# Gathered rows spread further into the V pass, and a final norm that takes some of its tokens as rows

## The chip, the cores and the metric

The kernel runs on one core of a Trainium2 chip. Its time is the device time of that core in microseconds; lower is better. Several executions are timed and their median is taken, and one execution is recorded by the hardware profiler. The engines are called PE (matrix products), ACT, DVE, POOL (GpSimd) and SP (which here only issues DMAs).

## The reference

The program is a decoder trunk of two layers over 256 tokens of width 1024. The even layer has an attention and a retention mixer, the odd layer a short gated convolution; each mixer is followed by a PEER block, and at the end stands a root-mean-square norm.

```
for layer in range(2):
    xn = rmsnorm(h, norm_mix[layer])
    h = h + (attn_retention_mixer if layer % 2 == 0 else short_conv_mixer)(xn, ...)
    h = h + peer(rmsnorm(h, norm_ffn[layer]), w_q, sub_keys, u, v)
return rmsnorm(h, final_norm)

# peer: per token, 8 heads each choose 16 of 16384 experts (product keys)
hid = gelu(einsum('td,thkd->thk', t, u[eidx]))
out = einsum('thk,thkd->td', gate * hid, v[eidx])

# short_conv_mixer
bg, cg, hx = split(xn @ w_in, 3);  return (bg * conv3(cg * hx)) @ w_out
```

All data are float32.

## The kernel before

**Two ways through PEER.** Each layer splits its 256 tokens. The last 160 (TD) go through all 16384 experts densely: the U pass multiplies 128 tiles of `pu` (128 experts x 1024, 512 KB each) into the hidden values HG, and the V pass multiplies 128 tiles of `pv` with HG into eight PSUM tiles `vo`, each holding 128 of the 1024 columns, transposed. The first 96 tokens (TG) are fetched: their 96 x 128 expert rows are gathered in 96 batches of 128 rows (512 KB) from `pun`, and again 96 from `pv`. One partition of a batch is one expert row. So a layer has 192 batches; the class `Gather` issues them by GpSimd's indirect DMA (L953) into six buffers, and consumes each with one DVE operation: L963 for the U half, L978 (L974 at two borders between quarters) for the V half, which adds the row, times its gate and hidden value, to an accumulator.

**The schedule of the batches.** `Gather.step` is called once a tile. It adds `rate` to a credit and, where the credit has reached one, consumes a batch and issues the next that has a free buffer. At the start of V, `rate` is set so that the batches left are used up after a fixed number of tiles (L1409). After the last batch GpSimd issues a small DMA (`part`, L990) that brings 32 partitions of an accumulator, 128 KB, to the others, and `fold` (L986, two DVE operations on 96 partitions) adds the accumulators to the residual `h`. The second of the two reads what the small DMA wrote. The fold stands at tile NK-5 = 123 of V.

**The tiles of V.** 95 of the 128 tiles are split (list SPL): ACT casts the tile to a rounded high half (L1356), DVE makes the remainder in bf16 (L1363), ACT and DVE do the same for the rows of HG (L1426, L1427, L1434; up to three tiles in one operation), and PE multiplies the halves (L1470, L1472). The other 33 go through in float32 (L1466). Casts run three tiles ahead of PE, remainders two. Raw tiles have eight buffers; even ones are issued by SP, odd ones by ACT. High and low halves have three buffers each. ACT, DVE, POOL and each DMA queue work in the order in which the program was written; nothing is moved by a planner.

**The end of V.** At tiles 16 to 23 PE adds the residual of the 160 dense tokens to `vo` by a product with the identity (L1455, L1456). At tile NK-2 = 126 it transposes the 96 fetched tokens of `h`, after the fold, into a free part of `vo` (L1458), and ACT copies them into the transposed residual XT (L1461). After tile 127 `fold(b)` (ACT L1479, DVE L1480) brings the dense tokens into XT. In the first layer XT feeds the odd mixer. In the last, `Final.folded` transposes XT back with PE (L504) into four tiles `fq`: quarters 0 and 1 are tokens 0 to 127, quarters 2 and 3 tokens 128 to 255. ACT sums the squares of each quarter (L579), DVE multiplies by the gain (L576), `mean0`, `root` and `rstd` (L363, L366, L371 to L375) make the scale of a half, `put` scales a quarter on DVE (L585) or ACT (L583), and SP sends it out (L586).

**The odd mixer.** Its 24 input tiles are split by the class `Stream`: ACT casts (L146) and the remainder is made by GpSimd or DVE (L148), by a flag beside each tile in `srcs`. Before the change GpSimd has the odd tiles from 7 on. PE multiplies the halves (L258, L264), and DVE does the gates and the convolution (L885 to L908).

Of the kernel before, what the change touches and what calls it, by code (L numbers as in the profile page):

```python
# [14 lines left out]
AF = mybir.ActivationFunctionType  # L15
OP = mybir.AluOpType
# [12 lines left out]
NK = 128  # L29
# [162 lines left out]
def trunk_kernel(ctx, tc, x, small, cst, mcst, ew_in, ew_out, ow_in, ow_out, wq, keys, pu, pv, pun, gains, out):  # L192
# [26 lines left out]
    srcs += [(ow_in[f], i > 6 and i % 2 == 1) for i, f in enumerate(OF)]  # L219
# [123 lines left out]
    class Sums:  # L343


        def __init__(self):
            self.w = pers.tile([P, 2, 8], F32, tag="nw", name=nm("nw"))
# [207 lines left out]
    class Final(Sums):  # L555


        def __init__(self, g):
            super().__init__()
            self.g = g  # L560
# [5 lines left out]
        def folded(self, XT, fold):  # L566

            xs = new_ko().rearrange("p (a d) -> p a d", a=2)
# [5 lines left out]

            def gained(a):
                v.tensor_tensor(part(a), fq[a], self.g[:, a % 2 * 512:(a % 2 + 1) * 512], OP.mult)  # L576

            def square(a):
                act.activation(junk, fq[a], AF.Square, accum_out=self.w[:, a // 2, a % 2:a % 2 + 1])  # L579
# [10 lines left out]
            for a in range(4):  # L590
                back(fq[a], XT, a // 2, a % 2)
            for a in range(2):
                square(a)
            self.mean0(0)
            self.root(0)
            gained(0)
            gained(1)
            self.rstd(0)
            for a in range(2, 4):
                square(a)  # L600
            self.mean0(1)
            self.root(1)
            put(0, v)
            gained(2)
            put(1, act)
            gained(3)
            self.rstd(1)
            put(2, v)
            put(3, act)
# [390 lines left out]
    def peer(l, before, norm):  # L1000
        with tc.tile_pool(name=nm("hg"), bufs=1) as hp:
# [407 lines left out]
            ga.rate = (ga.TOTAL - ga.c) / (NK - 10.0)  # L1409
# [29 lines left out]
            for i in range(NK):  # L1439
# [12 lines left out]
                for b in range(ND):  # L1452
                    c = slice(b * P, (b + 1) * P)
                    if i == 16 + b:
                        pe.matmul(vo[b][:, :P - TG], h[:, 0, c], ident[:, TG:], **m)  # L1455
                        pe.matmul(vo[b][:, P - TG:TD], h[:, 1, c], ident, **m)  # L1456
                    if i == NK - 2:
                        pe.matmul(vo[b][:, 2 * TD:2 * TD + TG], h[:, 0, c], ident[:, :TG], **m)  # L1458
                if i == NK - 2:
                    for b in range(ND):  # L1460
                        act.copy(XT[:, b, :TG], vo[b][:, 2 * TD:2 * TD + TG])  # L1461
# [13 lines left out]
                if i == NK - 5:  # L1475
                    assert ga.c == ga.TOTAL
                    ga.fold()
# [65 lines left out]
```

## Time and profile before

| | us |
|---|---|
| median of 3 runs | 1500.05 (1498.83 to 1500.72) |
| the profiled execution, its own time | 1498.47 |
| its span, from the first to the last instruction | 1496.7 |
| V pass of the first layer, PE's first to last product | 488.2 to 756.3 |
| V pass of the second layer | 1215.2 to 1485.5 |

The engines were busy for 1437.2 us (PE), 1251.9 (DVE), 762.7 (ACT) and 729.4 (POOL) of the span. A row of the profile that groups instructions has the line, engine, operation, output and inputs, shape and count, then busy time, the mean of one in ns, and the idle time before them with what ended it. A row of the timeline has start, duration, engine, line, and in brackets the idle time ahead of the instruction with its releaser. A row of a stretch has its limits and length, each engine's busy time with the number of instructions, the granted PE clock as a share, DMA's share and GB/s. A row of the chain has the start, the duration and what the end was waiting for at that time.

### The profile page before, as it was taken

What the parts mean: (1) busy time and instruction counts of PE and PEld (TensorE: products, weight loads), DVE (VectorE), ACT (ScalarE), POOL (GpSimd) and SP (SyncE); (2) the same over time, 40 slices, a digit from 0 to 9 for tenths busy, and PEclk for the clock granted to TensorE, in tenths of its full rate; (3) what the DMA queues carried; (4) which work ended last, traced back from release to release, by engine and by line L of the source; (5) the groups of instructions that cost most, each with busy time, mean ns of one, the idle gap of its engine ahead of it and who ended that gap; (6) DMA issues with size and microseconds to landing.
All of it is one profiled execution on the core that took longest, in us unless ns stands there. A gap on an engine that the chain in (4) does not pass through costs nothing.

```text
span 1496.7 us, 30119 instructions
## 1 busy us (share of the span) xinstructions
PE 1437.2 (96%) x11174; PEld 1336.0 (89%) x11188; DVE 1251.9 (84%) x2469; ACT 762.7 (51%) x1833; POOL 729.4 (49%) x512
## 2 busy tenths in 40 slices
PE   9999999999999999889999999999999999998897
PEld 5667999999999998888888799999999999988886
DVE  5637999879998888888877589996899969888886
ACT  6556512257885544445564463112888744444445
POOL 6754545446666344444125374454666725444430
PEclk9999999999999999999999999999999999999999
DMA  8545899999999999999966488999999999999994
GB/s 322 195 153 200 302 392 408 395 409 405 407 402 408 407 400 409 409 400 408 371 224 200 169 284 327 408 407 397 408 407 401 408 396 407 401 409 400 409 408 170
DMA packets 147570, 532.99 MB, mean 356 GB/s; under 512 B 16992, under 2 KB 17248, under 8 KB 147424
## 3 DMA queue, kind: packets, MB, share of 16 engines
q1 hardware_dynamic: 72144, 258.36, 45.2%
q0 software_dynamic: 56704, 205.07, 34.7%
q10 hardware_dynamic: 18576, 67.64, 11.5%
q8 instruction: 88, 1.44, 0.4%
q14 instruction: 58, 0.48, 0.1%
HBM read 528.34 MB, written 1.05 MB: 354 GB/s over the span
## 4 chain that ended last, share of the span: by engine, by line
PE 47%; DMA 27%; DVE 19%; issue 5%; ACT 3%; POOL 0%; SPq 0%; DVEq 0%; ACTq 0%; POOLq 0%
PE hid L1345 17%; DMA raw<-pv 12%; PE vo L1470 6%; DMA rows<-pun,ig 4%; PE vo L1466 4%; DMA grow<-pv,ig 4%; DMA rows<-pv,ig 3%; PE hid L258 3%; PE vo L1472 3%; DVE rows L963 3%; PE ea L290 2%; PE ea L291 2%; DVE gacc L978 2%; PE ea L292 1%; PE hid L264 1%
## 5 line engine op out<-in xcount | busy, mean ns | idle before, releaser
L1345 PE MATMUL hid<-xf,raw 128*128 128x160 f32 x3392 | 486.6, 301 | 6.3 <-DMA raw<-pu 4.0
L1345 PEld LDWEIGHTS hid<-xf,raw 128*128 128x128 f32 x3392 | 467.0, 191 | 8.9 <-issue 5.6
L1356 ACT CAST vhi<-raw 128x1024 fp32r<-128x1024 f32 x190 | 198.5, 1046 | 272.4 <-DMA raw<-pv 218.2
L1470 PE MATMUL vo<-ko,vhi 128*128 128x320 f32 x1520 | 271.6, 321 | 33.2 <-DVE ko L1434 32.8
L953 POOL DMA_INDIRECT rows<-pv,ig x128 | 186.2, 1455 | 214.0 <-DVE gacc L978 174.7
L1363 DVE TENSOR_TENSOR vlo<-raw,vhi 128x1024 bf16<-128x1024 f32 x190 | 231.5, 1222 | 63.9 <-ACT vhi L1356 51.0
L1470 PEld LDWEIGHTS vo<-ko,vhi 128*128 128x128 f32 x1520 | 225.4, 189 | 41.4 <-DVE ko L1434 40.2
L953 POOL DMA_INDIRECT rows<-pun,ig x128 | 171.1, 1337 | 133.9 <-DVE rows L963 61.7
L148 POOL TENSOR_TENSOR lo<-raw,hi 128x1024 bf16<-128x1024 f32 x68 | 163.4, 2416 | 76.9 <-ACT hi L146 74.0
L963 DVE SCALAR_TENSOR_TENSOR rows<-rows,xg 128x1024 f32<-128x1024 f32 x128 | 155.1, 1217 | 20.9 <-DMA rows<-pun,ig 18.5
L1378 ACT ACTIVATE hg<-hid 128x160 f32<-128x160 f32 (+14 forms) x240 | 62.4, 264 | 213.0 <-PE hid L1345 179.5
L978 DVE SCALAR_TENSOR_TENSOR gacc<-rows,ghid,gacc 128x1024 f32<-128x1024 f32 x124 | 158.6, 1279 | 12.9 <-DMA rows<-pv,ig 11.7
L1466 PE MATMUL vo<-hg,raw 128*128 128x160 f32 x1056 | 157.3, 302 | 0.8 <-DVE hg L1381 0.7
L1466 PEld LDWEIGHTS vo<-hg,raw 128*128 128x128 f32 x1056 | 145.5, 190 | 1.3 <-DVE hg L1381 1.3
L953 POOL DMA_INDIRECT grow<-pv,ig x64 | 98.2, 1534 | 98.9 <-DVE gacc L978 85.8
L1472 PE MATMUL vo<-hb,vlo 128*128 128x160 bf16 x1520 | 138.7, 235 | 0.2 <-DVE vlo L1363 0.2
L1472 PEld LDWEIGHTS <-vlo 128*128 128x128 bf16 x1520 | 101.0, 98 | 19.8 <-DVE vlo L1363 0.4
L953 POOL DMA_INDIRECT grow<-pun,ig x64 | 80.5, 1258 | 78.1 <-DVE grow L963 44.5
L1295 ACT ACTIVATE ko<-ko,idxT 128x128 f16<-128x128 f16 x320 | 101.7, 391 | 32.1 <-DVE ko L1281 29.7
L146 ACT CAST hi<-raw 128x1024 fp32r<-128x1024 f32 x100 | 102.4, 1047 | 17.4 <-issue 10.1
L258 PE MATMUL hid<-x,hi 128*128 128x256 f32 x800 | 107.4, 287 | 4.0 <-DVE cg L894 2.5
L258 PEld LDWEIGHTS hid<-x,hi 128*128 128x128 f32 x800 | 98.6, 190 | 5.0 <-ACT hi L146 2.7
(243 smaller groups left out, 2092.3 us busy)
## 6 DMA issues: line engine op xcount, KB each, us to landing
raw<-pu SPq DMA_DIRECT2D x212, 512.0 KB
raw<-pv SPq DMA_DIRECT2D x128, 512.0 KB
raw<-pv ACTq DMA_DIRECT2D x128, 512.0 KB
raw<-wq SPq DMA_DIRECT2D x32, 512.0 KB
raw<-ew_in SPq DMA_DIRECT2D x28, 512.0 KB
raw<-ow_in SPq DMA_DIRECT2D x24, 512.0 KB
hg<-pu SPq DMA_DIRECT2D x22, 512.0 KB
raw<-ew_out SPq DMA_DIRECT2D x8, 512.0 KB
```

Of the source, the lines that this page charges most:

```text
L146: self.nc.scalar.copy(hi, t)
L148: eng.tensor_tensor(lo, t, hi.bitcast(F32), OP.subtract)
L258: pe.matmul(ps[:, :S], hi[:, k * P:(k + 1) * P], A2[:, k, s_, :], start=k == 0 and s_ == 0, stop=False)
L953: gp.indirect_dma_start(self.row(s_), None, table, bass.IndirectOffsetOnAxis(IG[:, 0, s_ % STEPS:s_ % STEPS + 1].bitcast(U32), 0))
L963: v.scalar_tensor_tensor(r, r, 1.0, XG[:, q % 2, :], op0=OP.mult, op1=OP.mult, accum_out=w)
L978: v.scalar_tensor_tensor(self.acc[q], r, w, self.acc[q], op0=OP.mult, op1=OP.add)
L1345: pe.matmul(ps[:, :TD], w[k], XF[:, k, :], start=k == 0, stop=k == ND - 1)
L1356: act.copy(whi[j], raw)
L1363: v.tensor_tensor(wlo[j], raw, whi[j].bitcast(F32), OP.subtract)
L1466: pe.matmul(vo[b][:, :TD], w[:, b * P:(b + 1) * P], HG[:, i, :], stop=False, **m)
L1470: pe.matmul(vo[b][:, :2 * TD], hi[:, b * P:(b + 1) * P], hs, stop=i == NK - 1, **m)
L1472: pe.matmul(vo[b][:, :TD], lo[:, b * P:(b + 1) * P], hb, stop=i == NK - 1, **m)
```

## The change

Three parts:

1. The batches of a layer that are left at V's start are spread over 122.5 tiles in the first layer and 124.5 in the second, instead of 118. The fold moves from tile 123 to tile 125 and 126. In the first layer the transposes of the fetched tokens and their copies move from tile 126 to tile 127, ahead of that tile's products.
2. In the second layer the fetched tokens are not transposed any more. They stay rows of `h`. The final norm transposes quarters 2 and 3 first and works on them first; from quarters 0 and 1 only the partitions 96 to 127 are copied into `h` (two DVE operations), and squares and gains of that half read `h` instead of PSUM. The order of the norm's steps changes with it.
3. In the odd mixer the remainders of input tiles 3 and 5 are made by GpSimd instead of DVE.

```
-    srcs += [(ow_in[f], i > 6 and i % 2 == 1) for i, f in enumerate(OF)]
+    srcs += [(ow_in[f], i > 1 and i % 2 == 1) for i, f in enumerate(OF)]
...
+            def row(a):
+                return fq[a] if a > 1 else h[:, 0, a * 512:(a + 1) * 512]
+
             def gained(a):
-                v.tensor_tensor(part(a), fq[a], self.g[:, a % 2 * 512:(a % 2 + 1) * 512], OP.mult)
+                v.tensor_tensor(part(a), row(a), self.g[:, a % 2 * 512:(a % 2 + 1) * 512], OP.mult)
 
             def square(a):
-                act.activation(junk, fq[a], AF.Square, accum_out=self.w[:, a // 2, a % 2:a % 2 + 1])
+                act.activation(junk, row(a), AF.Square, accum_out=self.w[:, a // 2, a % 2:a % 2 + 1])
...
             for b in range(ND):
                 fold(b)
-            for a in range(4):
+            for a in (2, 3, 0, 1):
                 back(fq[a], XT, a // 2, a % 2)
+            for a in (2, 3):
+                square(a)
+            for a in range(2):
+                v.tensor_copy(h[TG:, 0, a * 512:(a + 1) * 512], fq[a][TG:, :])
+            self.mean0(1)
+            self.root(1)
+            gained(2)
+            gained(3)
+            self.rstd(1)
             for a in range(2):
                 square(a)
             self.mean0(0)
             self.root(0)
+            put(2, v)
             gained(0)
+            put(3, act)
             gained(1)
             self.rstd(0)
-            for a in range(2, 4):
-                square(a)
-            self.mean0(1)
-            self.root(1)
             put(0, v)
-            gained(2)
             put(1, act)
-            gained(3)
-            self.rstd(1)
-            put(2, v)
-            put(3, act)
...
-            ga.rate = (ga.TOTAL - ga.c) / (NK - 10.0)
+            last = norm.own
+            ga.rate = (ga.TOTAL - ga.c) / (NK - (3.5 if last else 5.5))
...
-                    if i == NK - 2:
+                    if i == NK - 1 and not last:
                         pe.matmul(vo[b][:, 2 * TD:2 * TD + TG], h[:, 0, c], ident[:, :TG], **m)
-                if i == NK - 2:
+                if i == NK - 1 and not last:
                     for b in range(ND):
                         act.copy(XT[:, b, :TG], vo[b][:, 2 * TD:2 * TD + TG])
...
-                if i == NK - 5:
+                if i == NK - (2 if last else 3):
                     assert ga.c == ga.TOTAL
                     ga.fold()
```

`last` is true for the norm at the end (`Final.own`), false for all others.

More of the change, by code (lines that the diff above doesn't have):

```diff
@@ L343, in trunk_kernel @@
     class Sums:
+        own = False
         def __init__(self):
@@ L555, in trunk_kernel @@
     class Final(Sums):
+        own = True
         def __init__(self, g):
```

## The prediction

> **What bounds the kernel now.** I read the page first (its span, busy times and the chain that ended last), then the busy times of chosen stretches of the second layer's V pass, then the chain and the timeline at the ends of both V passes.
>
> ```profile
> span 1496.7 us, 30119 instructions
> PE 47%; DMA 27%; DVE 19%; issue 5%; ACT 3%; POOL 0%; SPq 0%; DVEq 0%; ACTq 0%; POOLq 0%
> ...
> 1302.40:1466.65 164.25, 147.39 (x1216) 137.44 (x1216) 139.94 (x128) 76.90 (x97) 66.74 (x48) 1.00 1.02 405
> 1466.65:1474.50 7.85, 7.85 (x66) 7.54 (x67) 6.71 (x7) 5.51 (x8) 0.53 (x1) 1.00 0.84 318
> 1474.50:1485.20 10.70, 10.70 (x95) 10.29 (x94) 5.68 (x6) 4.00 (x13) 0.00 (x0) 1.00 0.01 3
> ...
> 1425.91 18.32 DMA rows<-pv,ig
> 1445.88 17.64 DMA rows<-pv,ig
> ```
>
> In the stretch rows PE comes first, then PEld, DVE, ACT, POOL, the clock, the DMA share and GB/s. From tile 43 of V (1302.40) to tile 119 (1466.65) DMA is full at 405 GB/s while PE has holes (147 of 164 us); a tile or a row batch of 524288 bytes costs 524288/405 GB/s = 1.29 us. From 1466.65 PE has none, and after 1474.5 DMA is empty. So one part of V waits for bytes, and its last 18 us for PE. The chain shows row batches that took 18 us from issue to landing, with six buffers in turn.
>
> **The rows.** How many batches V consumes follows from the accumulations in it:
>
> ```profile
> 488.00:742.50 254.50, 94.75 (x74) 0.99 1.02 402
> 1215.00:1471.50 256.50, 97.23 (x76) 1.00 1.02 403
> ...
> L974 DVE SCALAR_TENSOR_TENSOR gacc<-rows,ghid,gacc 96x1024 f32<-96x1024 f32 x4 | 5.1, 1275 | 1.3 <-DMA rows<-pv,ig 1.3
> ```
>
> With the two of L974 in each layer these are 76 and 78 batches of 192. The old rate is 76/118 = 0.644 and 78/118 = 0.661 a tile; the new one 76/122.5 = 0.620 and 78/124.5 = 0.627. The last batch is consumed at tile 119 now; counted with the credit that is carried in, it will be at 124 in the first layer and 126 in the second.
>
> ```profile
> 1453.22 1.68 POOL L953 DMA_INDIRECT rows<-pv,ig  x1 [0.65 <-DVE gacc L978]
> 1466.65 1.43 PE L1470 MATMUL vo<-ko,vhi 128*128 128x320 f32 x8 [1.70 <-DVE ko L1434]
> 1469.98 1.28 DVE L978 SCALAR_TENSOR_TENSOR gacc<-rows,ghid,gacc 128x1024 f32<-128x1024 f32 x1
> 1471.55 0.53 POOL L990 DMA_DIRECT2D gacc<-gacc  x1 [16.65 <-DVE gacc L978]
> 1472.05 2.38 PE L1466 MATMUL vo<-hg,raw 128*128 128x160 f32 x16
> 1475.64 1.05 ACT L1356 CAST vhi<-raw 128x1024 fp32r<-128x1024 f32 x1 [0.62 <-PE vo L1470]
> 1476.38 2.47 DVE L986 TENSOR_TENSOR h<-gacc,h 96x1024 f32<-96x1024 f32 x2
> 1479.57 1.96 PE L1458 MATMUL vo<-cst,h 128*128 128x96 f32 x16
> 1481.37 2.37 PE L1466 MATMUL vo<-hg,raw 128*128 128x160 f32 x16
> 1485.35 1.94 DVE L1480 TENSOR_TENSOR xg<-vo,xg 128x160 f32<-128x160 f32 x8 [5.13 <-ACT xg L1479]
> ```
>
> Second layer: up to tile 119, 115 steps have consumed 0.0346 x 115 = 4 batches fewer, at most 4 x 1.29 = 5.2 us of a full DMA. But six are then in flight where two were, partly carried for nothing; I count three batches: -3.9 us (bounds -2.6 for two, -5.2). After it PE goes on at (1481.37 - 1472.05 - 1.80)/4 = 1.88 us a tile. The transposes of the fetched tokens go from this layer: 1481.37 - 1479.57 = -1.8. The eight copies behind them are ACT's, beside PE. So the final additions (1485.35) could start at 1479.6.
>
> What is late next is the last batch. Its issue at 1453.22 moves five steps on (5 x 164.25/76 = 10.8) and 3.9 back: about 1460, or 1458 where DVE no longer waits for an earlier batch. Its consumption followed 16.8 us later, after the tile before it on DVE; landing at about 15 gives 1473 to 1475; I take 1474.5, and 1475.8 for the end of its accumulation. Then follow the small transfer (L990) and two halves of the fold, the second behind that transfer:
>
> ```profile
> L986 DVEq EVENT_SEMAPHORE  x2: 21/21/21, 748.8 to 1475.1; - x2
> ```
>
> That row gives its landing: 1475.1 - 1471.55 = 3.5 us here, 748.8 - 742.41 (below) = 6.4 in the first layer. 1475.8 + 3.5 + 1.2 = 1480.5 against 1479.6: +0.9 (bounds 0 and +4.8, the latter by the 18.3 us of the chain's row). Queued behind the fold on DVE are only the additions; the parts of tile 127 are ahead of it. The Trainium skill, DMA: Bandwidth & Descriptors, section on the anatomy of one DMA by the GpSimd path, gives 2.0 us plus the bytes over 436 GB/s; as an estimate 2.3 us for these 131072 bytes, and 0.9 would be 0. The rows here, 3.5 and 6.4, say more.
>
> **First layer's end.** Here the fold must precede PE's transposes, which now stand ahead of tile 127 instead of 126:
>
> ```profile
> 723.38 1.67 POOL L953 DMA_INDIRECT rows<-pv,ig  x1 [2.36 <-DVE gacc L978]
> 742.41 0.53 POOL L990 DMA_DIRECT2D gacc<-gacc  x1 [17.35 <-DVE gacc L978]
> 744.89 2.43 DVE L1363 TENSOR_TENSOR vlo<-raw,vhi 128x1024 bf16<-128x1024 f32 x2 [1.07 <-ACT vhi L1356]
> 747.55 1.05 ACT L1356 CAST vhi<-raw 128x1024 fp32r<-128x1024 f32 x1 [1.49 <-DMA raw<-pv]
> 748.89 1.22 DVE L986 TENSOR_TENSOR h<-gacc,h 96x1024 f32<-96x1024 f32 x1 [0.44 <-DMA gacc<-gacc]
> 750.36 1.96 PE L1458 MATMUL vo<-cst,h 128*128 128x96 f32 x16
> 752.15 2.37 PE L1466 MATMUL vo<-hg,raw 128*128 128x160 f32 x16
> 754.25 1.44 PE L1470 MATMUL vo<-ko,vhi 128*128 128x320 f32 x8
> ```
>
> Already now the fold ends (750.1) just before PE asks for it (750.36). Up to tile 111 there are 107 x 0.0237 = 2.5 batches fewer, 3.3 us; I take 2.7 at the end. PE would want the transposes at 750.36 - 2.7 + 2.1 = 749.8 (2.1 is tile 126, 754.25 - 752.15, which now goes ahead of them). The last batch is consumed behind the remainder of tile 125 (ends 747.3 now; I take 1.6 earlier, as ACT's casts hold it): 745.7 + 1.3 = 747.0. The transfer lands 3.5 to 6.4 us later, 752.0 between them, and the second half of the fold ends at 753.2; the first half, behind the cast (747.55), remainder and row rest of tile 127, ends earlier. Transposes 753.3, tile 127 at 755.1 instead of 754.25: +0.8. Behind the waiting fold DVE has a remainder of the odd mixer's first tiles, and one cast now stands behind the eight copies: +0.3. So the first layer loses 1.1 (bounds -1.6, with 3.5 us and all of 2.7; +4.2, with 6.4 and nothing of it).
>
> **The odd mixer.** Tiles 3 and 5 (DVE at 768.77 and 773.08) go to GpSimd:
>
> ```profile
> 768.77 1.23 DVE L148 TENSOR_TENSOR lo<-raw,hi 128x1024 bf16<-128x1024 f32 x1
> 770.68 1.22 DVE L148 TENSOR_TENSOR lo<-raw,hi 128x1024 bf16<-128x1024 f32 x1 [0.69 <-ACT hi L146]
> 773.08 1.22 DVE L148 TENSOR_TENSOR lo<-raw,hi 128x1024 bf16<-128x1024 f32 x1
> 779.16 5.72 POOL L148 TENSOR_TENSOR lo<-raw,hi 128x1024 bf16<-128x1024 f32 x2 [0.62 <-ACT hi L146]
> 780.00 2.63 DVE L148 TENSOR_TENSOR lo<-raw,hi 128x1024 bf16<-128x1024 f32 x1 [1.14 <-ACT hi L146]
> 788.63 2.14 PE L258 MATMUL hid<-x,hi 128*128 128x256 f32 x16 [2.48 <-DVE cg L894]
> ```
>
> The first is worth nothing: the next on DVE waits 0.69 for ACT anyway. The second lies on the chain by which PE waits 2.48 at 788.63: -1.1. Against it, an operation of DVE took 2.63 instead of 1.22 while GpSimd did the same (780.00), and GpSimd's of 2.9 (5.72 for two) runs from 768.8 to 771.6 and so over the start of tile 4's at 770.68: +0.6 (at most 1.4). Net -0.5 (bounds -1.1, +0.3). On POOL's queue the loading of the keys moves behind the first of them; its reader comes after the mixer. The Trainium skill, SBUF — State Buffer, section Who interferes with whom, says that a VectorE instruction with both inputs in SBUF contends with a GpSimd one that reads SBUF, and that the loser blocks until the other ends. This trace agrees: 2.63. By that rule tile 4's operation starts at 771.6, +0.9, and the net is -0.2 instead of -0.5.
>
> **The final norm.** From the first addition to the last scaling it is now 1492.48 - 1485.35 = 7.1 us:
>
> ```profile
> 1485.73 2.82 PE L504 MATMUL fq<-cst,xg 128*128 128x128 f32 x16 [0.26 <-DVE xg L1480]
> 1487.59 0.69 DVE L576 TENSOR_TENSOR ko<-fq,xf 128x512 f32<-128x512 f32 x1
> 1489.10 0.15 DVE L371 SCALAR_TENSOR_TENSOR nw<-nw 128x1 f32<-128x1 f32 x1
> 1489.99 0.48 DVE L585 TENSOR_SCALAR ko<-ko,nw 128x512 f32<-128x512 f32 x1
> 1492.48 0.72 ACT L583 ACTIVATE ko<-ko,nw 128x512 f32<-128x512 f32 x1 [1.46 <-DVE nw L375]
> ```
>
> After, on DVE, counted from the first addition: the two copies of 32 rows wait for the third and fourth transposed quarters (PE ends at +3.2; the third is there at +2.8) and take no row of this trace; between the 0.15 of a step on one column and the 0.69 of a 512-wide operation from PSUM, which they are nearest to, I take 0.6 each: until +4.0. All of the first half's arithmetic is queued behind them: mean 0.15, two gains of 0.69, the five small steps 0.9 (1489.10 to 1489.99), a mean 0.15, scaling 0.48, two gains of 0.6 from SBUF, the five steps 0.9, each overlapping a little: +8.5. The output transfers on SP go in the order of the scalings, the last behind the last one, as now. So the tail is +1.4 (bounds +0.5, +1.6).
>
> **The sum.** First layer +1.1, odd mixer -0.5, second layer -3.9 - 1.8 + 0.9, tail +1.4: -2.8. The profiled execution took 1498.47 us (1.77 around its span), so 1495.7. The median of the three runs, 1500.05, lies 1.58 above it: 1497.2 us. All bounds at one end give -9.2 and +6.5.
>
> **Rivals.** (1) The rows come last and set both ends: the last batch takes the 18.3 us of the full stretch, not 15. Second layer: 1460 + 18.3, consumed 1479.6, transfer and fold 1484.4, additions at 1484.5 instead of 1485.35; with the tail, +0.5. First layer: issued five tiles later (723.4 + 10 - 2.7 = 730.7), landing 749.0, fold 755.1, tile 127 at 757.0: +2.8 and 0.3. With -0.5: +3.1, and +6 with 6.4 us for one transfer: 1503 to 1506. It decides where the second layer's last batch lands after 1475, the first's after 746. For it speak six batches in flight to the end; against it that the stretch rows leave DMA only 84% busy before 1474.5, so that the same bytes could end earlier. (2) The folds hide: transfers of 3.5 us, four batches' worth saved: -1.6 - 0.5 - 5.2 - 1.8 + 1.4 = -7.7, 1492.4. (3) Bytes do not set V's pace; the six buffers' round trip and DVE's order do, and the rate brings nothing while both folds still come later. First layer: 747.3 + 1.3 + 5.0 + 1.2 = 754.8, tile 127 at 756.7, +2.7 in all. Second layer: the cast of tile 127 ends at 1476.7, its remainder and rest, the last batch, transfer and fold follow until 1484.2, a gain of 1.1 on 1485.35, less the tail's 1.4. With -0.5: +2.5, 1502.6. Against it stand 405 GB/s throughout.
>
> **How the numbers follow.** No change is what lies within 0.2% (3.0 us), about what a measurement can tell here. My forecast has 0.50, from 1494.5 to 1499.5, three fifths of it below 1497.05; rival (1) 0.20, (2) 0.15, (3) 0.15. Faster: 0.30 + 0.15 = 0.45. Slower, above 1503.05: 0.16 of (1) and 0.05 of (3). Same: the rest, 0.20 + 0.04 + 0.10 = 0.34. The range runs from just above the middle of (2), 1493, to 1504, where half of (1) ends, and leaves out some 0.19.
>
> **What would show it.** Right: PE reaches tile 119 of the second layer about 4 us earlier with DMA at 405 GB/s; the second fold of layer one starts about 752 and PE idles 3 us before L1458; no L1458 at the end; the tail 1.4 longer. Wrong: PE waiting inside tiles 119 to 127 for raw tiles, a last batch after 1476, a first-layer fold ahead of 750, or a DVE operation of 2.6 where tile 4's stood.

## The result, and the profile after

The changed kernel took 1502.99 us (median of 15 runs, 1500.61 to 1505.31) beside 1499.79 us for the kernel before (15 runs, 1498.82 to 1503.00): a ratio of 1.0020, with a 95% interval of 1.0012 to 1.0028. A second measurement (e13 below) gave 1.0020 again, 1.0011 to 1.0030. The forecast was 1497.2 us and faster; the time lies inside its range of 1493 to 1504, on the wrong side of no change.

The profiled execution took 1502.57 us, with this span and this chain:

```profile
span 1500.8 us, 30090 instructions
PE 49%; DMA 29%; DVE 9%; issue 8%; ACT 3%; POOL 2%; ACTq 0%; SPq 0%; DVEq 0%; POOLq 0%
```

PE has 49% of the chain instead of 47%, DVE 9% instead of 19%, and "issue" 8% instead of 5%. Most of that growth is two stretches of 19.9 and 19.3 us in which the chain runs through GpSimd's queue up to the small transfers, one in each layer. The span is divided here by PE's first and last products of each stage; the last two limits are the first final addition on DVE and the span's end.

| stage, us | before | after | difference |
|---|---|---|---|
| up to the first layer's V | 488.16 | 488.33 | +0.2 |
| V of the first layer | 268.10 | 270.87 | +2.8 |
| odd mixer and queries, to the second U pass | 154.94 | 155.89 | +0.9 |
| U of the second layer | 303.97 | 302.95 | -1.0 |
| V of the second layer, to the first final addition | 270.19 | 268.82 | -1.4 |
| tail, to the span's end | 11.36 | 13.95 | +2.6 |
| span | 1496.71 | 1500.81 | +4.1 |

The profiled spans lie 4.1 apart where the medians lie 3.2 apart. One of the stages, U of the second layer, has no edit in it; the 1.0 there is the execution's own: the kernel before has PE at a clock of 0.50 for 3.41 us of it, from 954.32, the changed kernel not at all, and e7, whose U pass is unedited too, took 302.95 again. In e13, the same kernel again, V of the second layer took 267.46. So a stage repeats to about a microsecond and a half, and a smaller difference between two single executions says little.

**Up to tile 119 the rates do what they should.** The busy times of stretches, from V's first product to tile 119, first layer and second, and the tail; the kernel before:

```profile
488.16:737.43 249.27, 233.92 (x1939) 220.56 (x1937) 212.91 (x197) 119.98 (x152) 105.51 (x72) 0.99 1.02 404
1215.16:1466.65 251.49, 232.70 (x1938) 219.09 (x1936) 215.67 (x199) 120.80 (x153) 104.83 (x74) 1.00 1.02 404
...
1485.35:1496.70 11.35, 2.94 (x18) 1.93 (x16) 6.95 (x26) 5.90 (x19) 0.00 (x0) 0.71 0.25 92
```

and the changed kernel, with the stretches behind tile 119 as well:

```profile
488.33:734.40 246.07, 232.81 (x1938) 219.15 (x1936) 209.57 (x194) 119.96 (x152) 102.73 (x72) 1.00 1.03 406
748.50:754.90 6.40, 2.82 (x22) 2.58 (x22) 4.80 (x5) 0.71 (x4) 0.53 (x1) 1.00 0.76 268
754.90:758.31 3.41, 3.41 (x17) 3.41 (x15) 0.49 (x2) 2.23 (x7) 0.00 (x0) 0.50 0.47 159
792.50:795.91 3.41, 3.41 (x18) 2.89 (x18) 2.16 (x4) 0.00 (x0) 0.22 (x1) 0.50 0.77 267
1218.04:1466.25 248.21, 233.16 (x1938) 219.11 (x1937) 211.03 (x194) 120.40 (x152) 102.77 (x74) 1.00 1.03 405
1466.25:1478.10 11.85, 11.64 (x98) 10.89 (x99) 10.00 (x9) 6.50 (x9) 0.00 (x0) 1.00 0.79 312
1478.10:1486.85 8.75, 5.83 (x48) 5.26 (x47) 7.42 (x8) 3.17 (x11) 0.53 (x1) 1.00 0.07 16
1486.85:1500.80 13.95, 3.33 (x16) 2.61 (x16) 8.32 (x29) 4.64 (x12) 0.00 (x0) 0.57 0.20 75
```

PE reaches tile 119 after 246.07 instead of 249.27 and after 248.21 instead of 251.49: 3.2 and 3.3 us earlier, at the same 405 GB/s. Then look at PE's busy time behind it. Before, PE was busy in all of the 10.70 us behind 1474.50, when the bytes had ended. Now bytes arrive until about 1478.1, and in the 8.75 us from there to the first addition PE has work for 5.83. In the first layer it has 2.82 of 6.40, and then 3.41 us at a granted clock of 0.50; the tail's clock is 0.57 instead of 0.71.

**The first layer's end**, in the timeline of the changed kernel (PE, DVE and POOL):

```profile
747.16 1.28 DVE L988 SCALAR_TENSOR_TENSOR gacc<-rows,ghid,gacc 128x1024 f32<-128x1024 f32 x1
747.86 2.38 PE L1477 MATMUL vo<-hg,raw 128*128 128x160 f32 x16
748.73 0.53 POOL L1000 DMA_DIRECT2D gacc<-gacc  x1 [19.93 <-DVE gacc L988]
752.55 1.22 DVE L996 TENSOR_TENSOR h<-gacc,h 96x1024 f32<-96x1024 f32 x1 [1.60 <-DMA gacc<-gacc]
753.82 2.75 PE L1469 MATMUL vo<-cst,h 128*128 128x96 f32 x16 [3.58 <-DVE h L996]
756.28 2.35 PE L1481 MATMUL vo<-ko,vhi 128*128 128x320 f32 x8
758.47 0.73 PE L1483 MATMUL vo<-hb,vlo 128*128 128x160 bf16 x8
```

PE has done tile 126 at 750.2 and stands 3.58 us before the transposes, which wait for the fold's second half, which waits for the small transfer. Then the clock halves: the transposes take 2.75 instead of 1.96 and tile 127's high half 2.35 instead of 1.44.

**The second layer's end**, same view, from the issue of the last batch on:

```profile
1463.23 0.94 POOL L963 DMA_INDIRECT rows<-pv,ig  x1 [0.65 <-DVE gacc L988]
...
1478.18 1.22 DVE L1373 TENSOR_TENSOR vlo<-raw,vhi 128x1024 bf16<-128x1024 f32 x1
1479.31 1.28 DVE L988 SCALAR_TENSOR_TENSOR gacc<-rows,ghid,gacc 128x1024 f32<-128x1024 f32 x1
1480.51 1.22 DVE L1373 TENSOR_TENSOR vlo<-raw,vhi 128x1024 bf16<-128x1024 f32 x1
1481.65 0.32 DVE L1445 TENSOR_TENSOR ko<-hg,ko 128x160 fp32r<-128x160 f32 x1
1481.88 1.28 DVE L988 SCALAR_TENSOR_TENSOR gacc<-rows,ghid,gacc 128x1024 f32<-128x1024 f32 x1
1483.19 1.22 DVE L996 TENSOR_TENSOR h<-gacc,h 96x1024 f32<-96x1024 f32 x1
1483.40 0.73 PE L1483 MATMUL vo<-hb,vlo 128*128 128x160 bf16 x8
1483.45 0.53 POOL L1000 DMA_DIRECT2D gacc<-gacc  x1 [19.28 <-DVE gacc L988]
1485.71 1.22 DVE L996 TENSOR_TENSOR h<-gacc,h 96x1024 f32<-96x1024 f32 x1 [1.30 <-DMA gacc<-gacc]
1486.85 1.93 DVE L1491 TENSOR_TENSOR xg<-vo,xg 128x160 f32<-128x160 f32 x8
1487.68 3.33 PE L506 MATMUL fq<-cst,xg 128*128 128x128 f32 x16 [3.56 <-DVE xg L1491]
1490.20 0.70 DVE L603 COPY h<-fq 32x512 f32<-32x512 f32 x1 [1.42 <-PE fq L506]
```

The last batch lands 15.3 us after its issue, at 1478.5. PE's last product of V is done at 1484.13. The additions (L1491) read only what PE made and what ACT copied, but DVE works in order, and ahead of them stand two consumptions, the remainder of tile 127, the rest of its rows, the two halves of the fold and between these 1.30 us of waiting for the small transfer. So they start at 1486.85, PE idles 3.56 us ahead of the norm's transposes, and these run at the lower clock (3.33 instead of 2.82).

### The profile page after: what moved, and what is told of

The parts are those of the page before. It is cut to its first block, busy times and chain, and to the rows that moved or that the text cites. A ratio compares the mean times of both kernels' runs of the same rounds, so it can differ in the third digit from the quotient of the medians.

```text
span 1500.8 us, 30090 instructions
## 1 busy us (share of the span) xinstructions
PE 1437.9 (96%) x11172; PEld 1336.0 (89%) x11172; DVE 1251.4 (83%) x2469; ACT 761.0 (51%) x1825; POOL 729.1 (49%) x514
## 3 DMA queue, kind: packets, MB, share of 16 engines
q8 instruction: 88, 1.44, 0.4%
HBM read 528.34 MB, written 1.05 MB: 353 GB/s over the span
## 4 chain that ended last, share of the span: by engine, by line
PE 49%; DMA 29%; DVE 9%; issue 8%; ACT 3%; POOL 2%; ACTq 0%; SPq 0%; DVEq 0%; POOLq 0%
PE hid L1355 28%; DMA raw<-pv 21%; PE hid L258 4%; DMA raw<-pu 4%; PE hid L264 2%; PE G L1315 2%; PE ea L292 2%; DMA rows<-pv,ig 2%; PE ea L291 2%; PE ea L290 2%; PE vo L1481 1%; POOL rows L963 1%; DVE gacc L988 1%; ACT hi L146 1%; PE vo L1477 1%
## 5 line engine op out<-in xcount | busy, mean ns | idle before, releaser
L963 POOL DMA_INDIRECT rows<-pv,ig x128 | 186.9, 1460 | 218.5 <-DVE gacc L988 181.1
L148 POOL TENSOR_TENSOR lo<-raw,hi 128x1024 bf16<-128x1024 f32 x70 | 168.0, 2414 | 82.8 <-ACT hi L146 80.6
L963 POOL DMA_INDIRECT grow<-pv,ig x64 | 91.0, 1422 | 107.4 <-DVE gacc L988 93.6
```

The lines of the kernel that those rows point to most:

```text
L148: eng.tensor_tensor(lo, t, hi.bitcast(F32), OP.subtract)
L963: gp.indirect_dma_start(self.row(s_), None, table, bass.IndirectOffsetOnAxis(IG[:, 0, s_ % STEPS:s_ % STEPS + 1].bitcast(U32), 0))
```

## The experiments

Four theories were set against each other. Q: the same bytes must come in either way, so the last raw tile and batch land no earlier, and the last batches, the transfer and the fold stand in DVE's order with PE behind them. N: the new order of the norm is the loss. C: the lowered clock behind PE's waits is the loss. P: the later places of fold and transposes are the loss, whatever the rate. Ratios are to the kernel before in the same measurement, whose median lay between 1499.8 and 1501.7; the difference of two of these ratios is uncertain by about 0.13%, 2 us. Stages are of one execution each.

| kernel | median, us | ratio (95%) | V, first layer | mixer | V, second layer | tail |
|---|---|---|---|---|---|---|
| changed | 1502.99 | 1.0020 (1.0012 to 1.0028) | 270.87 | 155.89 | 268.82 | 13.95 |
| e1 part 1 alone | 1508.58 | 1.0049 (1.0034 to 1.0063) | 272.43 | 154.65 | 275.09 | 11.37 |
| e2 part 2 alone | 1501.60 | 1.0007 (0.9998 to 1.0016) | 268.06 | 154.97 | 268.42 | 13.15 |
| e3 part 3 alone | 1500.13 | 0.9994 (0.9985 to 1.0003) | 268.62 | 154.32 | 270.57 | 11.38 |
| e4 changed, PE kept busy | 1500.56 | 1.0002 (0.9993 to 1.0011) | 269.61 | 156.58 | 267.08 | 13.96 |
| e5 changed, old rate | 1500.79 | 1.0001 (0.9992 to 1.0011) | 268.83 | 155.06 | 268.02 | 13.16 |
| e6 changed, copies later | 1502.06 | 1.0003 (0.9994 to 1.0012) | 271.28 | 154.02 | 268.91 | 13.31 |
| e7 before, four batches less | 1495.95 | 0.9960 (0.9947 to 0.9973) | 268.51 | 156.51 | 265.62 | 11.37 |
| e8 changed, no last transfer | 1500.67 | 0.9991 (0.9983 to 1.0000) | 268.33 | 156.65 | 267.52 | 14.00 |
| e9 first layer as before | 1500.08 | 0.9996 (0.9987 to 1.0005) | 268.61 | 155.86 | 268.13 | 13.32 |
| e10 both rates as before | 1499.37 | 0.9990 (0.9981 to 0.9999) | 268.39 | 154.33 | 267.90 | 12.85 |
| e11 e9, fold behind additions | 1497.77 | 0.9978 (0.9969 to 0.9987) | 268.52 | 154.31 | 264.60 | 14.59 |
| e12 e11 and first layer's rate | 1496.44 | 0.9964 (0.9952 to 0.9977) | (below) | (below) | 264.82 | 14.60 |
| e13 changed, again | 1503.99 | 1.0020 (1.0011 to 1.0030) | 270.48 | 155.91 | 267.46 | 14.29 |
| e14 changed, second fold moved | 1501.54 | 1.0005 (0.9996 to 1.0014) | 271.89 | 156.28 | 264.81 | 14.72 |

Five medians lie above what was expected: e1 by 2.1 us, e2 by 0.9, e8 by 0.7, e5 by 0.3, e3 by 0.1.

**e1 to e3: the three parts alone.** e1 has the rates and places of part 1 with the old norm, so the second layer keeps its transposes, at tile 127:

```
-ga.rate = (ga.TOTAL - ga.c) / (NK - 10.0)
+ga.rate = (ga.TOTAL - ga.c) / (NK - (3.5 if last else 5.5))
...
-if i == NK - 2:
+if i == NK - 1:
...
-if i == NK - 5:
+if i == NK - (2 if last else 3):
```

The second pair stands at the transposes and at their copies, the third at the fold.

> Part 1 alone: the rates and the later folds, with the old norm and the transposes kept in both layers (tile 127). Theory Q (the folds come last: the bytes of V are the same, so the last raw tiles land no earlier, and the last accumulations, the small transfer and the fold stand in line on DVE with PE behind them): the first layer's V ends 2.5 to 3 us later, the second's waits for its fold too, +2 to +4 more; 1504 to 1506.5. Rival N (the rows gain what was forecast, the new norm loses it): V of the second layer ends 3 to 4 us earlier; 1497 to 1500. Rival C (only the lowered PE clock behind the wait costs): +1.6 in the first layer, -3 in the second; about 1498.5.

The largest loss of all runs, +0.49%. The timeline of e1 at the second layer's end:

```profile
1489.20 3.73 PE L1462 MATMUL vo<-cst,h 128*128 128x96 f32 x16 [4.60 <-DVE h L989]
```

PE waits 4.60 us for the fold in this layer too, and the transposes behind it run at the lower clock (3.73 instead of 1.96). Part 1 by itself costs 4 to 5 us in each V pass: Q's order, with C's price on top.

e2 has part 2 with the old rate, the fold at tile 123 and the first layer's transposes at 126:

```
-ga.rate = (ga.TOTAL - ga.c) / (NK - (3.5 if last else 5.5))
+ga.rate = (ga.TOTAL - ga.c) / (NK - 10.0)
...
-if i == NK - (2 if last else 3):
+if i == NK - 5:
```

> Part 2 alone: the fetched tokens stay rows in the second layer, with the old rate, the fold at tile 123 and the transposes of the first layer at 126. Theory Q: V of the second layer ends 1.8 earlier (no transposes), the norm is 1.4 to 2.6 longer: 1499.5 to 1500.7. Rival N: +3 or more: 1502.5 to 1504. Rival C: no wait of PE, so as Q with the smaller tail: 1499.5.

The transposes that go are worth 1.8 us of V (268.42 for 270.19), the tail gets 1.8 longer (13.15 for 11.36): they cancel, and N isn't the main cause. e3 changes only the flag in `srcs` (`i > 6` to `i > 1`).

> Part 3 alone: remainders of the odd mixer's tiles 3 and 5 by GpSimd. All theories: PE reaches the ninth input tile 0.5 earlier; -0.5 within +-1: 1498.8 to 1500. Were it the cause of the loss, 1502 or more.

The stage is 0.6 shorter, too little for the median to show.

**e4: the clock.** In the changed kernel 60 small products of zeros go to PE between tile 126 and the first layer's transposes, into a part of `vo` that nobody reads:

```
                     if i == NK - 1 and not last:
+                        for _ in range(60 if b == 0 else 0):
+                            pe.matmul(vo[b][:, 2 * TD + TG:], Z[:, :P], Z[:, :P - SUB], **m)
                         pe.matmul(vo[b][:, 2 * TD:2 * TD + TG], h[:, 0, c], ident[:, :TG], **m)
```

> The changed kernel with 60 further small products on PE (into unused columns of a PSUM tile) ahead of the first layer's transposes, where PE now waits 3.6 us for the fold; the fold is not sooner. Rival C (the clock's drop behind that wait is the loss): transposes take 1.96 instead of 2.75, tile 127 1.44 instead of 2.35, -1.6 us: about 1501.2. Theory Q: the same, but this is 1.6 of some 6 us only, the rest stays. If the products end after the fold does, they cost up to 1 us themselves; if the clock drops for another reason, 1503.

Timeline of e4:

```profile
750.46 2.71 PE L1470 MATMUL vo<-z 128*128 128x96 bf16 x60
754.14 2.02 PE L1471 MATMUL vo<-cst,h 128*128 128x96 f32 x16 [0.97 <-DVE h L996]
757.20 0.73 PE L1485 MATMUL vo<-hb,vlo 128*128 128x160 bf16 x8
```

With PE idle for 0.97 us the clock stays. From the transposes' start to V's end it is 3.79 us (754.14 to 757.93), 5.38 in the changed kernel (753.82 to 759.20): the lowered clock costs 1.6 us up to V's end. Little of it reaches the next stage. The odd mixer's first product comes 271.17 us after V's start in e4, 271.66 in the changed kernel and 271.27 in e13: it waits for 1.55 us in e4 and for 0.80 in the others, because DVE's additions then stand behind a remainder of the mixer's first tiles (e5 shows this order). So C is at most a small part of the loss; the wait for the fold is still there, filled with zeros. The ratio fell by more (1.0020 to 1.0002), and no stage that e4 edits accounts for that.

**e5: the places without the rates.** The changed kernel with `NK - 10.0` in the rate; fold and transposes stay late.

> The changed kernel with the old rate (118 tiles) in both layers: the last batch is back at tile 119, and only the places of the folds (tiles 125 and 126) and of the transposes stay late. Theory Q (the late last batch holds the fold): PE no longer waits in front of the transposes, the first layer's V within 0.5 of before; the second's 1.8 shorter, the norm 1.8 longer, the mixer -0.5: 1499 to 1500.5. Rival P (the fold's place behind tile 127's parts is enough to make PE wait): 2 to 3 more, 1502 to 1503.

Timeline of e5, first layer and second:

```profile
754.71 1.92 PE L1469 MATMUL vo<-cst,h 128*128 128x96 f32 x16
757.89 1.23 DVE L148 TENSOR_TENSOR lo<-raw,hi 128x1024 bf16<-128x1024 f32 x1 [3.26 <-ACT hi L146]
759.94 1.26 PE L275 MATMUL hid<-x,hi 128*128 128x256 f32 x6 [1.54 <-ACT x L522]
...
1486.02 2.36 PE L506 MATMUL fq<-cst,xg 128*128 128x128 f32 x16 [0.72 <-DVE xg L1491]
```

There is no wait for the fold, and no lower clock at these two places: the waits come with the new rates. But P isn't quite nothing. With the transposes late, ACT's copies of the fetched tokens (L1472) come late too, a cast of the odd mixer stands behind them, and DVE makes its remainder (L148) ahead of the additions. The mixer's first product comes 1.54 us after V's end, where it was 0.80 before: 270.4 us after V's start, for 268.9 to 269.4 in the kernels with the old places. The prediction had 0.3 for this cast and remainder.

**e6: the order in the norm.** The changed kernel with the two copies (L603) behind the gains of quarters 2 and 3.

> The changed kernel with the two copies of 32 rows moved behind the gains of quarters 2 and 3. If the copies at the head of DVE's line cost their wait (1.4 and 0.2 us idle ahead of them in the changed kernel), the tail is 1.2 to 1.6 shorter, about 1501.5. If the tail is longer for its own instructions alone (the copies' 2 x 0.70), it stays, 1503.

The tail is 0.6 shorter (13.31 for 13.95), half of what was expected if the place of the copies were the price. The median differs by more, which this study doesn't account for.

**e7: the price of a batch.** The kernel before with the second layer's last four batches left out (`ga.TOTAL -= 4 * l`).

> The kernel before, with the last four row batches of the second layer left out (its output lacks four experts' share of each fetched token). It prices a batch. If bytes set V's pace up to tile 119 and nothing behind it does, 4 x 1.29 = 5.2 us less: 1495. If only part of V is bound by bytes, 2 to 4 less. If the round trip of the six buffers sets it (20 us for six), 0.034 batches a tile fewer over 76 tiles at 3.3 us: 8 to 9 less.

V of the second layer is 4.57 us shorter, 1.14 a batch, where the prediction had 1.29; the 8 to 9 us of the buffers' round trip are ruled out. By itself this doesn't tell the bytes from DVE, since consuming a batch takes DVE 1.28 us. The stretches do: up to tile 119 DMA is full at 404 GB/s, while DVE is busy for 215.67 of 251.49 us. So bytes set V's pace, and the rate moves bytes; it doesn't remove any.

**e8: the small transfer.** The changed kernel without the last `part(2)`.

> The changed kernel without the last small transfer of either layer (a third of one accumulator's upper partitions is left out of the fold), so that the fold's second half waits for nothing. Theory Q (the wait for that transfer is one part of the line): first layer 1.6 earlier, and if PE's wait then stays under 2 us its clock does not drop, another 1.6; second layer 1.3 earlier; together -3 to -4.5, 1498.5 to 1500. If the DVE's own line alone holds the fold, less than 1 us.

In its timeline PE's wait at the first layer's end is 1.88 instead of 3.58, and the clock stays through tile 127 (these transposes take 2.02):

```profile
753.29 2.02 PE L1467 MATMUL vo<-cst,h 128*128 128x96 f32 x16 [1.88 <-DVE h L994]
```

2.5 us of V come back in the first layer, and 1.8 at the mixer's first product (269.88 us after V's start for 271.66). In the second, the additions start 1.46 us after PE's last product instead of 2.72 (1486.85 less 1484.13; the same 2.72 in e13), so the wait for the transfer is 1.3 of that. The transfer is about half of each wait; the other half is DVE's line without it.

**e9 and e10: one rate at a time.** e10 is what is left when both rates, the fold's and the transposes' places go back: part 2 with the copies behind the gains, and part 3. From e10 to e9 only the second layer's new rate and late fold come in:

```
-ga.rate = (ga.TOTAL - ga.c) / (NK - 10.0)
+ga.rate = (ga.TOTAL - ga.c) / (NK - (3.5 if last else 10.0))
...
-if i == NK - 5:
+if i == NK - (2 if last else 5):
```

> The changed kernel with the first layer's rate, fold and transposes as before the change (rate over 118 tiles, fold at tile 123, transposes at tile 126); the second layer keeps the new rate over 124.5 tiles, the fold at tile 126 and the rows in the norm, with the two copies behind the gains of quarters 2 and 3; tiles 3 and 5 of the odd mixer stay with GpSimd. Theory Q (the same bytes; the last raw tile lands no earlier, the last batch, transfer and fold stand behind it): first layer's V 268.1 to 268.6 as before, second layer's V up to the first addition 268.5 to 269.5, the tail 13.3: 1499.5 to 1500.5. If the rate were worth its batches in the second layer (3.9 us, as I predicted): second layer's V 265.5, 1496.5.

> The same kernel with the second layer's rate and fold put back as well (118 tiles, tile 123): what is left of the change is the norm on rows, its copies behind the gains, no transposes in the second layer, and tiles 3 and 5 on GpSimd. Theory Q: second layer's V 268.0 to 268.8 (the 1.8 us of the transposes, nothing from the rate), the tail 12.4 to 12.9, mixer 0 to 0.5 shorter: 1498.5 to 1500, so no slower than with the new rate in the second layer. If the rate were worth its batches: 2 to 3 us slower than that kernel.

V of the second layer: 268.13 with the new rate, 267.90 without. The 3.9 us of the prediction aren't there. The timeline of e9 says where they went:

```profile
1481.69 0.73 PE L1483 MATMUL vo<-hb,vlo 128*128 128x160 bf16 x8
1484.00 1.22 DVE L996 TENSOR_TENSOR h<-gacc,h 96x1024 f32<-96x1024 f32 x1 [1.30 <-DMA gacc<-gacc]
1485.15 1.92 DVE L1491 TENSOR_TENSOR xg<-vo,xg 128x160 f32<-128x160 f32 x8
1485.97 3.28 PE L506 MATMUL fq<-cst,xg 128*128 128x128 f32 x16 [3.56 <-DVE xg L1491]
```

PE ends at 1482.42, 265.40 us after V's start (268.02 in e10, by its 1215.28 to 1483.30): PE did get 2.6 us. The additions start 2.73 later, behind the fold.

**e11 and e12: the fold out of the way.** If that order is the cause, nothing but the place of the fold on DVE has to change. In e11, which is otherwise e9, the second layer's fold stands behind the additions and the issue of the norm's transposes:

```
-                if i == NK - (2 if last else 5):
+                if i == NK - 5 and not last:
                     ga.fold()
...
+            norm.rows = ga.fold
             norm.folded(XT, fold)
...
             for a in (2, 3, 0, 1):
                 back(fq[a], XT, a // 2, a % 2)
+            self.rows()
```

e12 adds the first layer's new rate and the fold at tile 125, with the transposes behind tile 127 instead of ahead of it, and the dense tokens' copies and additions ahead of the fetched ones' copies:

```
+            if not last:
+                for b in range(ND):
+                    pe.matmul(vo[b][:, 2 * TD:2 * TD + TG], h[:, 0, b * P:(b + 1) * P], ident[:, :TG], **m)
+                for b in range(ND):
+                    act.copy(XT[:, b, TG:], vo[b][:, TD:2 * TD])
+                    v.tensor_tensor(XT[:, b, TG:], vo[b][:, :TD], XT[:, b, TG:], OP.add)
             def fold(b):
+                if not last:
+                    act.copy(XT[:, b, :TG], vo[b][:, 2 * TD:2 * TD + TG])
+                    return
```

> The kernel of e9_layer1_old (first layer's V as before the change; new rate over 124.5 tiles in the second layer; copies of the norm behind the gains; tiles 3 and 5 on GpSimd) with one move: in the second layer the fold stands on DVE behind the additions of the dense tokens and the issue of the norm's transposes, instead of ahead of them. Nothing that these additions read depends on the fold. Theory Q with its last step (the rate's gain reaches PE, and is lost because the additions stand on DVE behind last batch, transfer and fold): the additions start when PE ends, 265.0 to 265.6 after V's start instead of 268.13; PE idles under 1 us ahead of the norm's transposes instead of 3.56 and these run at full clock; the fold's 2.4 us lie in DVE's wait for the squares and the tail is 12.8 to 13.3: 1496.5 to 1498, about 2 us less than e10_both_old. If instead the bytes alone set the end of the second layer, nothing moves: 1499.5 to 1500.5.

> The kernel of e11_fold_behind with the first layer's new rate (122.5 tiles) and the fold at tile 125 as in the changed kernel, but the transposes of the fetched tokens behind the products of tile 127 instead of ahead of them, and the copies and additions of the dense tokens ahead of the copies of the fetched ones. Theory: in the changed kernel PE had tile 127 ready and waited 3.58 us for the fold ahead of it, and lost its clock for 3.41 us. Here tile 127 ends about 752.4, PE waits 1 to 1.5 us and does the transposes at 753.5 to 754.0 at full clock; the odd mixer's first product comes at 756.5 to 757.5 instead of 759.99, where e9_layer1_old has it at about 758. So 0 to 1.5 us less than e11_fold_behind: 1495.5 to 1497.5. If the bytes set the first layer's end however the fold is placed: the same as e11_fold_behind or 1 us more.

Timeline of e11 at the end:

```profile
1479.92 1.94 DVE L1492 TENSOR_TENSOR xg<-vo,xg 128x160 f32<-128x160 f32 x8 [0.85 <-ACT xg L1491]
1480.76 2.35 PE L506 MATMUL fq<-cst,xg 128*128 128x128 f32 x16 [0.72 <-DVE xg L1492]
1481.78 2.47 DVE L997 TENSOR_TENSOR h<-gacc,h 96x1024 f32<-96x1024 f32 x2
1484.17 0.14 DVE L365 TENSOR_SCALAR nw<-nw 128x1 f32<-128x1 f32 x1
```

DVE now waits for ACT and PE ahead of the additions, not the other way round; PE idles 0.72 us, and its transposes take 2.35. V is 3.5 us shorter than in e9. The expected tail was wrong: the fold's 2.47 us aren't hidden in a wait for the squares, the mean (L365) stands behind them, and the tail is 14.59, not 12.8 to 13.3. Net, 1497.77 against 1500.08, and 0.9978 against 0.9996 as ratios: the rate's gain comes out once nothing stands in front of it. Against e10, which has the old rate, V is 3.3 shorter and the tail 1.7 longer; the two ratios' intervals overlap, so what the rate is worth net stays uncertain.

In e12 PE's wait at the first layer's end is 1.76, behind all of V, and the first product of the mixer comes at 758.39, 269.8 us after V's start, where the changed kernel has 759.99 (271.7); 756.5 to 757.5 was expected:

```profile
754.67 2.35 PE L1488 MATMUL vo<-cst,h 128*128 128x96 f32 x16 [1.76 <-DVE h L997]
758.39 4.15 PE L275 MATMUL hid<-x,hi 128*128 128x256 f32 x16 [1.37 <-ACT x L522]
```

PE's clock halves all the same, at 756.21 and for 6.83 us (4.15 for 16 products, with 2.15 for the next 16), which was not expected. e12 is the best of all: 1496.44 us, 0.36% below the kernel before. The intervals of e12 and e11 overlap as ratios, but the two were timed together, and the means of their runs are 1496.2 and 1498.1.

**e13 and e14: the loss again, and the one move in the changed kernel.** e13 is the changed kernel without an edit; e14 is the changed kernel with the move of e11 alone.

> The changed kernel itself, without an edit, timed beside the kernel before on another chip. Its ratio was 1.0020 [1.0012, 1.0028] when it was first measured; kernels one edit away from it (filler on PE, copies of the norm moved, no last transfer) were at 1.0002, 1.0003 and 0.9991 in other measurements, which by their stages is 1 to 2 us less than the edits account for. If the loss is the kernel's own: 1.0010 to 1.0025. If part of it belonged to the chip or to where the lowered clock happened to fall: 1.0000 to 1.0010.

> The changed kernel with one move: in the second layer the fold stands on DVE behind the additions of the dense tokens, as in e11_fold_behind; the first layer and the order of the norm's copies stay as changed. Theory Q with its last step: second layer's V up to the first addition 264.6 to 265.5 instead of 268.82, PE idles under 1 us ahead of the norm's transposes; the fold's 2.4 us then stand in the tail on DVE, 14.5 to 16 from the first addition; net 2 to 3.5 us less than e13_changed_again. If the additions were held by something else: no change.

e13 repeats the 0.2%, so it is the kernel's own. Its timeline has the wait, 2.95 us here, and the lowered clock at the same place:

```profile
753.79 2.80 PE L1469 MATMUL vo<-cst,h 128*128 128x96 f32 x16 [2.95 <-DVE h L996]
```

e14, timed together with e13, takes 2.45 us less (1501.54 for 1503.99): V of the second layer falls to 264.81, the tail grows to 14.72. The first layer's V, which this kernel leaves as changed, is still 3.8 us longer than in the kernel before.

## Why the prediction was wrong, step by step

By terms, forecast and measured: first layer +1.1 and +2.8, odd mixer -0.5 and +0.9, second layer's V -4.8 and -1.4, tail +1.4 and +2.6. The largest miss is the second layer's V.

**What bounds V: right.** Bytes do, at 405 GB/s; a batch is worth 1.14 us (e7; 1.29 forecast).

**"The rows": this step failed.** The gain up to tile 119 was right in size (3.3 us for 3.9), and the last batch was issued and landed nearly where it was forecast: issued at 1463.23, which is 1460.35 in the prediction's time (V starts 2.88 later), for 1460, and landed 15.3 us later, at 1475.7, for 1474.5. Wrong was the step that follows, by which the end of its accumulation comes 1.3 us after the landing, at 1475.8. It ended at 1483.16, or 1480.3: DVE is at work without a pause from 1478.18 to the fold, and had two remainders, a consumption and the rest of tile 127's rows to do first. "Landing" was taken for "consumed", which put the accumulation 4.5 us too early. The transfer then was shorter than forecast (2.2 us from issue to landing in the second layer, 3.7 in the first, for 3.5 and some 5):

```profile
gacc<-gacc POOLq DMA_DIRECT2D x1, 128.0 KB, 2.2
```

The estimate of 2.3 us, which the prediction gave and set aside, comes near the 2.2. Even so the fold ended at 1484.05 of the prediction's time instead of 1480.5. So the term was not -3.9 and +0.9 but -2.6 at PE and nothing at the additions (e9 against e10); -1.8 for the transposes was right (e2), and 268.82 less 270.19 is about what they give. By the prediction's working the fold is 0.9 behind PE; it is 2.8 behind (1486.93 less 1484.13). e11 and e14, which take the fold out of DVE's way and change no byte, give 2.6 to 4.0 us of V back, and that is what shows the cause.

**"First layer's end": the fold's time came out by luck, the clock was missing.** The fold's second half was forecast to start at 752.0 and started at 752.55; transposes at 753.3, measured 753.82. Two errors cancel in it: the last accumulation ended at 748.4 instead of 747.0, the same step as above, and the transfer took 3.7 instead of 5.0. Tile 127 was to come at 755.1 and came at 756.28, and V's end moved by 2.8, not 0.8: 1.6 of the difference is the clock that PE loses after its wait (e4). The prediction even named the wait ("PE idles 3 us") and gave it no price. At the mixer's first product 2.8 stands against the forecast 1.1; there e4, without the lowered clock, is no more than 0.5 better, because the cast and remainder that the prediction put at 0.3 then hold the additions. The Trainium skill, TensorE: Matmul & The Clock Gate, section HAM oscillation — how this bites in real kernels, states as a rule that PE should have no idle gaps above about 3.4 us, since it runs at half rate after one; the trace agrees in the 0.50, but not in the limit: e13's clock fell after a wait of 2.95 us, and e12's after one of 1.76.

**"The odd mixer": right.** From V's end to the product that waits 2.48 us for DVE it is 31.7 us in the changed kernel, 31.8 in e10 and 32.4 before: -0.6 for -0.5. The next rows show why the stage is longer all the same:

```profile
771.82 2.38 POOL L148 TENSOR_TENSOR lo<-raw,hi 128x1024 bf16<-128x1024 f32 x1 [5.42 <-ACT hi L146]
773.63 1.65 DVE L148 TENSOR_TENSOR lo<-raw,hi 128x1024 bf16<-128x1024 f32 x1 [2.06 <-ACT hi L146]
790.94 2.53 PE L258 MATMUL hid<-x,hi 128*128 128x256 f32 x16 [2.46 <-DVE cg L904]
793.27 1.93 PE L264 MATMUL hid<-xb,lo 128*128 128x256 bf16 x8
```

Tile 4's remainder took 1.65 instead of 1.22 beside GpSimd's, as forecast; but behind the 2.46 us wait, which was there before, the clock halves at 792.50 (the row above), and products of 1.05 take 1.93. It fell there in e9 and e13 too, and not in e10 and e11, whose wait is the same. It also fell in e7, which has the kernel before's mixer unedited (156.51 for 154.94), so these 1.5 us can't be put down to the change. What differs is how the wait lies in time. In every trace here the clock changes only on a grid of 3.41 us, which lies otherwise in each execution. The steps of it with most of the 2.46 to 2.48 us wait, in the kernel before and in the changed one:

```profile
787.06:790.47 3.41, 1.83 (x15) 1.87 (x16) 3.20 (x6) 1.73 (x2) 2.49 (x1) 1.00 0.60 208
789.06:792.47 3.41, 1.53 (x13) 1.56 (x14) 3.02 (x6) 2.03 (x3) 2.25 (x1) 1.00 0.54 207
```

PE is busy for 1.53 us of the step in the changed kernel, 1.46 in e13 and 0.93 in e7 and e9, and the next step has 0.50; it is busy for 1.83 before, 1.82 in e11 and 1.66 in e10, and the clock stays. That is read from the traces; no run moved the wait against the grid on purpose.

**"The final norm": mis-sized.** +1.4 was forecast, +2.6 measured. With the transposes at full clock it is +1.8 (e2, e5). The copies take 0.70 each instead of 0.6, and wait for PE; the other 0.8 is the lower clock of the transposes behind PE's 3.56 us wait, which follows from the fold being late.

**The rivals.** The number came out as in the third, 1502.6, and by similar terms: first layer 2.7 (2.8 measured), second layer -1.1 (-1.4). But its reason, that bytes do not set V's pace and the rate brings nothing, is refuted: PE was 3.3 us earlier at tile 119, and the 8 to 9 us of its round trip didn't come in e7. Its number is luck. Nearest in the order of things is the first one, with the rows last at both ends: additions at 1484.5 in the prediction's time, measured 1484.0. But that agrees by luck too, for its last batch takes 18.3 us where 15.3 was measured, and DVE's line made up the difference. It was given 0.20, because the forecast let the rows end earlier in the holes that DMA had behind tile 119 (84% busy); the holes stayed, 79% busy from tile 119 to the last byte.

## What to carry to other kernels

When a resource is full, delaying optional bytes brings the needed ones forward only until the last of them; then all that follows the optional bytes (here two consumptions, a transfer, a fold) stands behind the end of the traffic, and it must be costed in the order of the engine that does it, from the landing of the last byte, instruction by instruction. Before moving a producer later, look for consumers that are queued behind it on the same engine without needing it: here one move of the fold took back most of what the change had lost (1.0020 to 1.0005). And price each new PE wait for the clock behind it as well as for its length, but do it where the next stage begins: 1.6 us of lowered clock at V's end were 0.5 at most at the mixer's first product.

## What the runs showed of the hardware

- With a PE wait of 2.95 to 4.60 us at the end of V the granted clock fell to 0.50 in every run that had one, for 3.41 us where PE went on working, in e1 for 6.83. Behind the 3.58 us wait this cost 1.6 us more up to V's end. Waits of 0.97 and 1.88 (e4, e8) left the clock alone up to there, one of 1.76 (e12) didn't; those of 2.46 to 2.48 in the mixer sometimes did and sometimes didn't, with nearly the same instructions around them.
- The clock changed only on a grid of 3.41 us. At the mixer's wait it fell where PE was busy for 1.53 us of a step or less, and stayed where it was 1.66 or more. Elsewhere the limit is less sharp: in e5 it fell at 762.33 behind a step with 2.09 us of work.
- The small transfer of 128 KB took 2.2 us when the queues were empty (second layer) and 3.7 beside the mixer's weights (first layer); in the kernel before, where it came earlier, 3.5 and 6.4.
- Copies of 32 partitions by 512 from PSUM took 0.70 us on DVE, as much as a two-input operation on 128 partitions by 512 (0.69 in the kernel before). No run has the same copy on 128 partitions.
